# Lp-pooling over 1024 windows of four: one square and one sum per load, pairwise adds at the end, and an early first store

## The chip, the cores and the metric

The kernel runs on one core of a Trainium2 chip. Its time is the device time of one execution in microseconds (us); lower is better. "Span" is the time from the first to the last instruction of an execution; the device time of the kernel before is about 1.8 us longer.

## The reference

The input has 32 x 256 x 4096 float32 values (134.2 MB). Each output is the root of the mean of four neighbouring squares; the output has 32 x 256 x 1024 values (33.6 MB).

```python
window = np.abs(x[:, :, start:end]) ** p            # p = 2, four values
result[:, :, i] = (np.mean(window, axis=-1)) ** (1.0 / p)
```

## The kernel before

The flat input is cut into 22 loads; each has 128 rows, and most have 13184 columns (6.75 MB). Three SBUF slots hold loads, so two are usually on their way while one is worked on. Such a load is worked on in three chunks (the smaller loads at the end in two): ScalarE squares a chunk in place, VectorE sums each four neighbours with one `tensor_reduce`, and ScalarE takes the root one chunk later. Results of two loads form a group, with one store (at the end there is one group of three loads and one of a single load). Groups 0 to 6 are stored from ScalarE's queue; groups 7 to 10 are "late": they are stored from SyncE's (SP) queue, behind the last load.

```python
W, O_W = 13184, 6592
X_SLOTS, O_SLOTS = 3, 2
slots = [[(W, [4416, 4384, 4384])]] * 18
slots += [[(6592, [3296, 3296])] * 2, [(6592, [3296, 3296]), (5056, [2528, 2528])]]
groups = [2] * 9 + [3, 1]
late = {7, 8, 9, 10}
in_x = {9, 10}          # these results lie in a slot that no load needs any more
# ... cut: offsets, pools, load(), store()
def root(g, o, ends):
    nc.scalar.activation(out=o, in_=o, func=Act.Sqrt, scale=1.0 / k)
    if ends and g not in late:
        store(g, nc.scalar)
# ... cut: for each load i, with further loads issued up to two slots ahead
    for step in chunks:
        v = xs[i][:, c:c + step]
        nc.scalar.activation(out=v, in_=v, func=Act.Square)
        o = ots[g][:, at + c // k:at + (c + step) // k]
        nc.vector.tensor_reduce(
            out=o, in_=v.rearrange("p (n j) -> p n j", j=k),
            axis=mybir.AxisListType.X, op=mybir.AluOpType.add,
        )
        if pending is not None:
            root(*pending)
        c += step
        pending = (g, o, i == firsts[g] + groups[g] - 1 and c == w)
root(*pending)
for g in sorted(late):
    store(g, nc.sync)
```

## Time and profile before

| | kernel before |
|---|---|
| device time, median of the first 3 runs | 394.89 us (394.77 to 394.97) |
| span of the profiled run | 393.0 us |
| bytes moved, mean rate over the span | 167.79 MB, 427 GB/s |
| VectorE, ScalarE busy | 282.4 us, 292.4 us |

DVE is VectorE, ACT is ScalarE, SP is SyncE, which here only issues DMAs. The page of the kernel before, with the busy time of each engine (share of the span, number of instructions), the DMA's rate in 40 equal slices, and the memory traffic:

```profile
span 393.0 us, 316 instructions
## 1 busy us (share of the span) xinstructions
DVE 282.4 (72%) x62; ACT 292.4 (74%) x126; POOL 0.2 (0%) x4
...
GB/s 344 429 429 440 429 424 381 443 459 429 413 440 435 429 427 432 429 440 441 437 448 421 432 462 435 392 429 472 429 413 451 425 429 429 424 429 427 438 429 329
...
HBM read 134.22 MB, written 33.55 MB: 427 GB/s over the span
...
```

Only the first and the last slice are low; the bytes are fixed by the input and the output. Next, busy time by stretches, kernel before (start and end in us, length, then busy us and instructions of each engine, clock, DMA share, GB/s):

```profile
...
core 0: us, DVE busy (x) ACT busy (x) POOL busy (x), PEclk, DMA share, GB/s
4.00:388.00 384.00, 282.36 (x62) 291.15 (x125) 0.00 (x0) 1.00 1.00 432
340.00:388.00 48.00, 43.61 (x12) 43.16 (x23) 0.00 (x0) 1.00 1.00 431
388.00:390.00 2.00, 0.00 (x0) 0.00 (x0) 0.00 (x0) 1.00 0.89 376
390.00:392.00 2.00, 0.00 (x0) 0.00 (x0) 0.00 (x0) 1.00 0.52 215
392.00:394.00 2.00, 0.00 (x0) 0.00 (x0) 0.00 (x0) 1.00 0.00 0
...
```

The rate is 432 GB/s through the whole middle and 431 at the end, so I read no stage as having a limit other than the DMA. Three lines of the timeline of the kernel before (start, duration, engine, line, operation, tiles and shapes, number of instructions merged, and what ended the idle time):

```profile
...
19.53 7.63 ACT L108 ACTIVATE xt<-xt 128x4416 f32<-128x4416 f32 x2 [17.52 <-DMA xt<-in_x_dram]
...
35.10 3.88 ACT L108 ACTIVATE xt<-xt 128x4416 f32<-128x4416 f32 x1 [0.75 <-DMA xt<-in_x_dram]
...
50.70 3.88 ACT L108 ACTIVATE xt<-xt 128x4416 f32<-128x4416 f32 x1 [1.02 <-DMA xt<-in_x_dram]
...
```

ScalarE starts when a load has landed, at 19.53, 35.10 and 50.70 us, one 6.75 MB load every 15.6 us. From the groups of instructions by shape (output shape, input shape, count; busy us, mean ns of one; idle time before them):

```profile
...
L110 DVE TENSOR_REDUCE ot<-xt 128x1096 f32<-128x4384 f32 x36 | 169.9, 4719 | 6.7 <-ACT xt L108 6.4
L108 ACT ACTIVATE xt<-xt 128x4384 f32<-128x4384 f32 x36 | 138.3, 3843 | 2.9 <-ACT ot L84 2.9
...
```

The last DMA issues of SP, from the timeline of the kernel before; "x2" merges two, one at the start and one at the end of the piece:

```profile
...
342.45 0.80 SPq L75 DMA_DIRECT2D xt<-in_x_dram  x2
343.30 16.29 SPq L81 DMA_DIRECT2D out_dram<-ot  x2
381.39 6.11 SPq L81 DMA_DIRECT2D out_dram<-xt  x2
```

So the four late stores are issued at 343.3, 359.2, 381.4 and 387.2 us. The chain that ended last, from the page of the kernel before:

```profile
...
DMA 62%; ACT 19%; DVE 14%; issue 2%; ACTq 0%; SPq 0%
DMA xt<-in_x_dram 62%; ACT xt L108 15%; DVE ot L110 11%; DVE xt L110 3%; ACT ot L84 3%; ACT xt L84 1%; ACTq L81 0%; SPq L75 0%; ACTq L108 0%
...
```

It names ScalarE and VectorE for a third of the span. The chain follows what released the last instruction; it doesn't say that shorter work would have ended earlier. The stretches above say that the DMA had no pause to give.

### The profile page before, as it was taken

What the parts mean: (1) busy time and instruction counts of PE and PEld (TensorE: products, weight loads), DVE (VectorE), ACT (ScalarE), POOL (GpSimd) and SP (SyncE); (2) the same over time, 40 slices, a digit from 0 to 9 for tenths busy, and PEclk for the clock granted to TensorE, in tenths of its full rate; (3) what the DMA queues carried; (4) which work ended last, traced back from release to release, by engine and by line L of the source; (5) the groups of instructions that cost most, each with busy time, mean ns of one, the idle gap of its engine ahead of it and who ended that gap; (6) DMA issues with size and microseconds to landing.
All of it is one profiled execution on the core that took longest, in us unless ns stands there. A gap on an engine that the chain in (4) does not pass through costs nothing.

```text
span 393.0 us, 316 instructions
## 1 busy us (share of the span) xinstructions
DVE 282.4 (72%) x62; ACT 292.4 (74%) x126; POOL 0.2 (0%) x4
## 2 busy tenths in 40 slices
DVE  0068989494959495949594959595859686899992
ACT  1099986777786768686958695959595949899991
POOL 0000000000000000000000000000000000000000
DMA  8999999999999999999999999999999999999997
GB/s 344 429 429 440 429 424 381 443 459 429 413 440 435 429 427 432 429 440 441 437 448 421 432 462 435 392 429 472 429 413 451 425 429 429 424 429 427 438 429 329
DMA packets 4754, 167.79 MB, mean 427 GB/s; under 512 B 528, under 2 KB 528, under 8 KB 656
## 3 DMA queue, kind: packets, MB, share of 16 engines
q1 hardware_dynamic: 3744, 144.15, 85.3%
q10 hardware_dynamic: 1008, 23.63, 14.0%
q14 instruction: 2, 0.02, 0.0%
HBM read 134.22 MB, written 33.55 MB: 427 GB/s over the span
## 4 chain that ended last, share of the span: by engine, by line
DMA 62%; ACT 19%; DVE 14%; issue 2%; ACTq 0%; SPq 0%
DMA xt<-in_x_dram 62%; ACT xt L108 15%; DVE ot L110 11%; DVE xt L110 3%; ACT ot L84 3%; ACT xt L84 1%; ACTq L81 0%; SPq L75 0%; ACTq L108 0%
## 5 line engine op out<-in xcount | busy, mean ns | idle before, releaser
L110 DVE TENSOR_REDUCE ot<-xt 128x1096 f32<-128x4384 f32 (+1 forms) x54 | 255.4, 4731 | 102.7 <-ACT xt L108 102.4
L108 ACT ACTIVATE xt<-xt 128x4384 f32<-128x4384 f32 (+3 forms) x62 | 230.3, 3716 | 89.2 <-DMA xt<-in_x_dram 86.3
L84 ACT ACTIVATE ot<-ot 128x1096 f32<-128x1096 f32 (+1 forms) x54 | 59.8, 1108 | 1.8 <-DVE ot L110 0.9
L110 DVE TENSOR_REDUCE xt<-xt 128x824 f32<-128x3296 f32 (+1 forms) x8 | 27.0, 3384 | 1.3 <-ACT xt L108 1.2
L84 ACT ACTIVATE xt<-xt 128x824 f32<-128x824 f32 (+1 forms) x8 | 6.7, 841 | 3.0 <-DVE xt L110 2.9
L108 ACT ACT_TABLE_LOAD x1 | 1.3, 1283 | 0.7 <-PEq L137 0.7
L84 ACT ACT_TABLE_LOAD x1 | 1.3, 1283 | 0.0
L137 POOL MEMSET const-bfloat16-1.0<- 128x1 bf16 x1 | 0.1, 101 | 0.0
L137 POOL MEMSET const-uint8-127<- 128x1 uint8 x1 | 0.1, 101 | 0.0
L137 POOL MEMSET const-float32-0.0<- 128x1 f32 x1 | 0.1, 98 | 0.2 <-issue 0.2
L137 POOL MEMSET const-float32-1.0<- 128x1 f32 x1 | 0.1, 98 | 0.0
## 6 DMA issues: line engine op xcount, KB each, us to landing
xt<-in_x_dram SPq DMA_DIRECT2D x18, 6592.0 KB, 39.7
out_dram<-ot ACTq DMA_DIRECT2D x7, 3296.0 KB, 26.4
xt<-in_x_dram SPq DMA_DIRECT2D x3, 3296.0 KB, 24.6
out_dram<-ot SPq DMA_DIRECT2D x2, 3296.0 KB, 29.6
xt<-in_x_dram SPq DMA_DIRECT2D x1, 2528.0 KB, 26.4
out_dram<-xt SPq DMA_DIRECT2D x1, 2472.0 KB, 9.3
out_dram<-xt SPq DMA_DIRECT2D x1, 632.0 KB, 5.0
```

Source lines behind the costliest of these rows:

```text
L84: nc.scalar.activation(out=o, in_=o, func=Act.Sqrt, scale=1.0 / k)
L108: nc.scalar.activation(out=v, in_=v, func=Act.Square)
L110: nc.vector.tensor_reduce(out=o, in_=v.rearrange("p (n j) -> p n j", j=k), axis=mybir.AxisListType.X, op=mybir.AluOpType.add,)
L137: nc = _bacc.Bacc("TRN2", target_bir_lowering=False, num_devices=1)
```

## The change

The intent is fewer, larger instructions: one square and one sum for a whole load; from load 16 on, two packed pairwise adds instead of the reduce; roots by group; and an early start: the first 4416 columns are squared on VectorE beside ScalarE, and their 1104 results are stored from SP ahead of their group. The tiles become fixed buffers (that part of the diff is cut).

```diff
-    slots = [[(W, [4416, 4384, 4384])]] * 18
-    slots += [[(6592, [3296, 3296])] * 2, [(6592, [3296, 3296]), (5056, [2528, 2528])]]
+    slots = [[(W, [4416, 8768])]] + [[(W, [W])]] * 16 + [[(W, [6592, 6592])]]
+    slots += [[(6592, [6592]), (6592, [6592])], [(6592, [6592]), (5056, [2528, 2528])]]
-    in_x = {9, 10}
+    in_x = {9: (2, 0), 10: (2, 4944)}
+    FINE, ENDS, LAG = {21}, {19}, 1
+    PAIRS = 16
 ...
+        elif g == 0 and not stored[g]:
+            store(g, nc.sync, o.shape[1])
+    def total_sum(o, v, i):
+        if i < PAIRS: ...            # the tensor_reduce, as before
+        q = v.rearrange("p (n j) -> p n j", j=k)
+        front = v[:, 0:v.shape[1] // 2]
+        h = front.rearrange("p (n j) -> p n j", j=2)
+        nc.vector.tensor_tensor(out=h, in0=q[:, :, 0:2], in1=q[:, :, 2:4], op=add)
+        nc.vector.tensor_tensor(out=o, in0=h[:, :, 0], in1=h[:, :, 1], op=add)
 ...
-            nc.scalar.activation(out=v, in_=v, func=Act.Square)
-            ... tensor_reduce, then root(*pending)
+            if i == 0 and c == 0:
+                nc.vector.tensor_tensor(out=v, in0=v, in1=v, op=mybir.AluOpType.mult)
+            else:
+                nc.scalar.activation(out=v, in_=v, func=Act.Square)
+            total_sum(ots[g][:, summed:summed + step // k], v, i)
+            while pending and pending[0][0] <= done - LAG:
+                root(*pending.pop(0)[1:])
 ...
+            ends = summed == columns[g] // k
+            if ends or i in FINE or (i == 0 and c == step) or (i in ENDS and c == w):
+                pending.append((done - 1, g, ots[g][:, rooted:summed], ends))
```

More of the change, by code (lines that the diff above doesn't have):

```diff
@@ L55 @@
                for g in range(len(groups))]
-    x_pool = ctx.enter_context(tc.tile_pool(name="x_pool", bufs=X_SLOTS))
-    o_pool = ctx.enter_context(tc.tile_pool(name="o_pool", bufs=O_SLOTS))
+    x_pool = ctx.enter_context(tc.tile_pool(name="x_pool", bufs=1))
+    o_pool = ctx.enter_context(tc.tile_pool(name="o_pool", bufs=1))
+    x_tiles = [x_pool.tile([P, W], fp32, name=f"xt{j}") for j in range(X_SLOTS)]
+    o_tiles = [o_pool.tile([P, O_W], fp32, name=f"ot{j}") for j in range(O_SLOTS)]
     ctx.enter_context(tc.manual_schedule())
@@ L63, in block @@
         return flat[at:at + width].rearrange("(p w) -> p w", p=P)
-    slot_tiles = {}
     xs = {}
@@ L69, in load @@
         s, at, w, _ = loads[i]
-        if at == 0:
-            slot_tiles[s] = x_pool.tile([P, W], fp32, name="xt")
-        v = slot_tiles[s][:, at:at + w]
+        v = x_tiles[s % X_SLOTS][:, at:at + w]
         g = group_of[i]
@@ L78, with store @@
     ots = {}
-    def store(g, queue):
-        queue.dma_start(out=block(of, g, k), in_=ots[g])
+    stored = [0] * len(groups)
+    def store(g, queue, end=None):
+        first, end = stored[g], columns[g] // k if end is None else end
+        queue.dma_start(out=block(of, g, k)[:, first:end], in_=ots[g][:, first:end])
+        stored[g] = end
     def root(g, o, ends):
@@ L86, in root @@
             store(g, nc.scalar)
+        elif g == 0 and not stored[g]:
+            store(g, nc.sync, o.shape[1])
+    def total_sum(o, v, i):
+        add = mybir.AluOpType.add
+        if i < PAIRS:
+            nc.vector.tensor_reduce(
+                out=o, in_=v.rearrange("p (n j) -> p n j", j=k),
+                axis=mybir.AxisListType.X, op=add,
+            )
+            return
+        q = v.rearrange("p (n j) -> p n j", j=k)
[3 more added lines that the diff above has]
+        nc.vector.tensor_tensor(out=o, in0=h[:, :, 0], in1=h[:, :, 1], op=add)
     ahead = 0
@@ L91 @@
         ahead += 1
-    pending = None
+    pending = []
+    done = 0
     for i in range(n):
@@ L99 @@
         if i == firsts[g]:
-            pool, width = (o_pool, O_W) if g not in in_x else (x_pool, W)
-            t = pool.tile([P, width], fp32, name="ot" if g not in in_x else "xt")
-            ots[g] = t[:, 0:columns[g] // k]
-        at = sum(loads[j][2] for j in range(firsts[g], i)) // k
+            t, first = (o_tiles[g % O_SLOTS], 0) if g not in in_x else (x_tiles[in_x[g][0]], in_x[g][1])
+            ots[g] = t[:, first:first + columns[g] // k]
+            summed = rooted = 0
         assert sum(chunks) == w
@@ L107 @@
             v = xs[i][:, c:c + step]
-            nc.scalar.activation(out=v, in_=v, func=Act.Square)
-            o = ots[g][:, at + c // k:at + (c + step) // k]
-            nc.vector.tensor_reduce(
-                out=o, in_=v.rearrange("p (n j) -> p n j", j=k),
-                axis=mybir.AxisListType.X, op=mybir.AluOpType.add,
-            )
-            if pending is not None:
-                root(*pending)
-            c += step
-            pending = (g, o, i == firsts[g] + groups[g] - 1 and c == w)
-    root(*pending)
+            if i == 0 and c == 0:
[5 more added lines that the diff above has]
+                root(*pending.pop(0)[1:])
+            done += 1
+            c += step
+            summed += step // k
+            ends = summed == columns[g] // k
+            if ends or i in FINE or (i == 0 and c == step) or (i in ENDS and c == w):
+                pending.append((done - 1, g, ots[g][:, rooted:summed], ends))
+                rooted = summed
+    for job in pending:
+        root(*job[1:])
     for g in sorted(late):
```

## The prediction

> What bounds the kernel now: the DMA, over the whole span. The page counts 167.79 MB in 393.0 us. The view of busy time by stretches gives 432 GB/s from 4 to 388 us at a DMA share of 1.00, 431 from 20 to 340 and from 340 to 388: no stage is slower. The timeline shows ScalarE starting on loads at 19.53, 35.10 and 50.70 us, one 6.75 MB load per 15.6 us (433 GB/s). The Trainium skill ("DMA: Bandwidth & Descriptors", section "Where 436 GB/s comes from") puts the ceiling at 435; the trace agrees within 1%.
>
> The chain of waits names ScalarE and VectorE for the last 47 us, but I read the end as DMA-bound too. The last stores are issued at 343.3, 359.2, 381.4 and 387.2 us; the last two land 9.3 and 5.0 us later, at 390.7 and 392.2. The second lands near 384.8 (landing median of the first two 29.6). So 2.53 MB takes 5.9 us and 0.65 MB 1.5, exactly the DMA rate: the stores stand in a queue, and the last results are ready 3.5 us before it reaches them.
>
> Floor: start 3.9 us (19.53 minus 15.6) plus 167.8 MB at 432 GB/s = 388.4 makes 392.3; the last store lands at 392.2. Nothing is left outside the DMA.
>
> What changes:
> - One square per load instead of three: 3 x 3.85 becomes about 11.2 us (slope 0.836 ns per column between the forms of 3296 and 4384). A slot is freed about 25 us after its load lands (11.2 square, 13.9 sum) instead of 18. Loads land every 19.6 us with two in flight, so the next load is still issued some 14 us before the queue runs dry.
> - First 4416 columns squared on VectorE (about 4.7 us): VectorE ends slot 0 near 38 us, as now. Their store, 0.57 MB, goes out near 30 us. It moves bytes forward in a queue that is full already, gaining nothing.
> - Packed pairwise adds in loads 16 to 21: two tensor_tensor instead of one reduce. The Trainium skill ("VectorE: DVE Perf Modes", section "The perf-mode tier table") has fp32 tensor_tensor at 1x, so I estimate 0.75 of the reduce: 6592 columns 5.3 us instead of 7.0.
> - Tail by my hand schedule: roots end near 386 to 387 us (now 387.15); store 9 ready near 381 to 382, store 10 near 386 to 387. Both find the queue occupied (until 384.8 and 390.7).
>
> On the critical path: none of it, to within 0.3 us. Bytes and DMA rate are unchanged.
>
> Predicted: 394.8 us, 8 in 10 within 393.9 to 395.9. Faster by over 2%: 0.01; within 2%: 0.96; slower by over 2%: 0.03.
>
> Signs that I am right: 431 to 433 GB/s from 4 to 388 us; first load used at 19.5; ScalarE and VectorE busy time down (VectorE by about 10 us net) with the span within 1 us; last stores landing back to back. Signs that a step is wrong: a stretch of several us under 420 GB/s (slots freed too late); pair adds over 0.8 of the reduce; the last store issued after its predecessor has landed.
>
> What would make it wrong: strided pair adds at half speed, which would push the tail by up to 10 us; false waits between reused tiles (the early store holding VectorE, stores holding later sums), draining the load queue; a DMA rate that depends on how reads and writes overlap, worth 1 us either way.

## The result

| | before | changed |
|---|---|---|
| device time, median of 6 runs | 394.92 us (394.77 to 395.22) | 395.65 us (395.36 to 395.86) |
| span of the profiled run | 393.0 us | 394.0 us |
| VectorE, ScalarE busy | 282.4, 292.4 us | 269.5, 277.9 us |

The ratio is 1.0017 (95% interval 1.0004 to 1.003). The page of the changed kernel, the same parts as before:

```profile
span 394.0 us, 198 instructions
## 1 busy us (share of the span) xinstructions
DVE 269.5 (68%) x34; ACT 277.9 (71%) x40; POOL 0.2 (0%) x4
...
GB/s 343 428 428 428 428 400 428 450 462 402 428 452 431 455 434 404 431 471 428 391 439 455 426 428 428 431 428 463 431 455 396 471 434 428 388 428 433 429 433 283
...
HBM read 134.22 MB, written 33.55 MB: 426 GB/s over the span
...
```

VectorE works 12.9 us less and ScalarE 14.5 us less, and the span of the profiled run is 1 us longer. Busy time by stretches, changed kernel:

```profile
...
4.00:388.00 384.00, 269.45 (x34) 276.61 (x39) 0.00 (x0) 1.00 1.00 432
340.00:388.00 48.00, 37.74 (x16) 44.74 (x13) 0.00 (x0) 1.00 1.01 433
388.00:390.00 2.00, 0.00 (x0) 0.00 (x0) 0.00 (x0) 1.00 0.88 372
390.00:392.00 2.00, 0.00 (x0) 0.00 (x0) 0.00 (x0) 1.00 0.42 172
392.00:394.00 2.00, 0.00 (x0) 0.00 (x0) 0.00 (x0) 1.00 0.02 8
...
```

From 4 to 388 us the DMA rate is again 432 GB/s. The timeline of the changed kernel, at the start:

```profile
...
19.50 7.51 ACT L134 ACTIVATE xt<-xt 128x8768 f32<-128x8768 f32 x1 [17.49 <-DMA xt<-in_x_dram]
19.50 4.76 DVE L132 TENSOR_TENSOR xt<-xt 128x4416 f32<-128x4416 f32 x1 [19.50 <-DMA xt<-in_x_dram]
...
30.23 0.35 SPq L86 DMA_DIRECT2D out_dram<-ot  x1
35.08 11.19 ACT L134 ACTIVATE xt<-xt 128x13184 f32<-128x13184 f32 x1 [4.87 <-DMA xt<-in_x_dram]
38.27 39.06 SPq L77 DMA_DIRECT2D xt<-in_x_dram  x3
...
```

The first load is used at 19.50 us on both engines at once, and the early store is issued at 30.23 us (by the trace's packet records its bytes move from 50.1 to 52.9 us, behind loads that stood in the queue already). The first slot is free again, and its next load is issued, at 38.27 us; before it was 38.12 us. The groups by shape, changed kernel:

```profile
...
L99 DVE TENSOR_REDUCE ot<-xt 128x3296 f32<-128x13184 f32 x15 | 208.3, 13886 | 80.2 <-ACT xt L134 80.2
L134 ACT ACTIVATE xt<-xt 128x13184 f32<-128x13184 f32 x16 | 179.0, 11190 | 87.8 <-DMA xt<-in_x_dram 86.6 <-ACT ot L90 1.2
...
L108 DVE TENSOR_TENSOR xt<-xt 128x3296 f32<-128x3296 f32 x5 | 18.0, 3593 | 6.5 <-ACT xt L134 6.3
...
L109 DVE TENSOR_TENSOR xt<-xt 128x1648 f32<-128x1648 f32 x3 | 5.6, 1874 | 0.1
L132 DVE TENSOR_TENSOR xt<-xt 128x4416 f32<-128x4416 f32 x1 | 4.8, 4759 | 19.5 <-DMA xt<-in_x_dram 19.5
...
```

The pairwise adds of 6592 columns take 3.59 + 1.87 = 5.47 us; the reduce of the same width took 7.01 us (measured in the run without pair adds, below). The last issues of SP, changed kernel:

```profile
...
346.01 0.80 SPq L77 DMA_DIRECT2D xt<-in_x_dram  x2
346.90 16.75 SPq L86 DMA_DIRECT2D out_dram<-ot  x2
381.63 5.65 SPq L86 DMA_DIRECT2D out_dram<-xt  x2
```

Store 9 is issued at 381.63 us and store 10 at 386.95 us, 0.24 us later and 0.22 us earlier than before.

Where, then, is the longer span? Every DMA reports its completion 16 times, once for each of the 16 DMA engines that share it. For the last store, in us from the start of the span, taken from the trace's completion records:

```
                       median engine   mean engine   last engine   last minus median
before                       391.62        391.63        392.22              0.60
changed                      391.29        391.46        393.12              1.83
changed, second run          391.33        391.41        392.60              1.26
```

The median and the mean engine end up to 0.3 us earlier than before. The last engine ends 0.4 to 0.9 us later, and the span ends with it. (The records don't name the engine, so it need not be the same one throughout.) In the changed kernel the last engine was 0.86 us behind the median at the first load, 1.26 us at the first load after the early store and 1.8 to 1.9 us from about 210 us on, apart from landings with another transfer in between. As long as the queue doesn't run empty, I read a lag as staying, unless the others lose time too; experiments 7 to 9, where the queue runs empty, bear this out (last section).

The step at the early store stands in all nine kept traces that have three slots and such a store: the lag grows by 0.16 to 0.54 us between the landings just before and just after its bytes. But it belongs to the first store of a run, early or not: in the three traces without an early store (before, experiments 1 and 2) the lag stays or falls there and grows by 0.2 to 0.4 us at their first store. The kernels part later: before, the lag falls by 0.5 us between 83 and 90 us; in the changed kernel it grows by another 0.66 us near 210 us, in experiment 2 by 1.0 us between 144 and 165 us. The traces show no cause for these steps.

### The profile page after: what moved, and what is told of

Its sections match the earlier page's. It is cut to its first block, busy times and chain, and to the rows that moved or that the text cites. A ratio compares the mean times of both kernels' runs of the same rounds, so it can differ in the third digit from the quotient of the medians.

```text
span 394.0 us, 198 instructions
## 1 busy us (share of the span) xinstructions
DVE 269.5 (68%) x34; ACT 277.9 (71%) x40; POOL 0.2 (0%) x4
## 4 chain that ended last, share of the span: by engine, by line
DMA 43%; ACT 28%; DVE 16%; issue 11%; ACTq 0%; SPq 0%
DMA xt<-in_x_dram 43%; ACT xt L134 20%; DVE ot L99 14%; ACT ot L90 7%; DVE xt L108 1%; DVE xt L109 1%; ACT xt L90 1%; ACTq L86 0%; SPq L77 0%; ACTq L90 0%
## 5 line engine op out<-in xcount | busy, mean ns | idle before, releaser
L134 ACT ACTIVATE xt<-xt 128x13184 f32<-128x13184 f32 (+3 forms) x24 | 219.2, 9147 | 105.3 <-DMA xt<-in_x_dram 104.1
L99 DVE TENSOR_REDUCE ot<-xt 128x3296 f32<-128x13184 f32 (+2 forms) x17 | 222.2, 13078 | 80.3 <-ACT xt L134 80.2
L90 ACT ACTIVATE ot<-ot 128x6592 f32<-128x6592 f32 (+2 forms) x10 | 51.3, 5134 | 0.8 <-DVE ot L99 0.8
L108 DVE TENSOR_TENSOR xt<-xt 128x3296 f32<-128x3296 f32 (+2 forms) x8 | 27.9, 3492 | 16.7 <-ACT xt L134 16.4
L132 DVE TENSOR_TENSOR xt<-xt 128x4416 f32<-128x4416 f32 x1 | 4.8, 4759 | 19.5 <-DMA xt<-in_x_dram 19.5
L90 ACT ACTIVATE xt<-xt 128x632 f32<-128x632 f32 (+2 forms) x4 | 6.0, 1493 | 2.2 <-DVE xt L109 2.1
L109 DVE TENSOR_TENSOR ot<-xt 128x1648 f32<-128x1648 f32 (+1 forms) x3 | 7.3, 2447 | 0.1
L109 DVE TENSOR_TENSOR xt<-xt 128x1648 f32<-128x1648 f32 (+1 forms) x5 | 7.3, 1452 | 0.2
```

Source lines behind the costliest of these rows:

```text
L99: nc.vector.tensor_reduce(out=o, in_=v.rearrange("p (n j) -> p n j", j=k), axis=mybir.AxisListType.X, op=add,)
L108: nc.vector.tensor_tensor(out=h, in0=q[:, :, 0:2], in1=q[:, :, 2:4], op=add)
L109: nc.vector.tensor_tensor(out=o, in0=h[:, :, 0], in1=h[:, :, 1], op=add)
L132: nc.vector.tensor_tensor(out=v, in0=v, in1=v, op=mybir.AluOpType.mult)
```

## The experiments

"Before" in each line is the kernel before, run on the same chip.

**1. The DMA alone.** All loads and stores stay, but the arithmetic handles only the last 64 columns of a chunk. The results are wrong (relative error 0.58); the result tiles are filled once at the start. There is no early store.

```diff
-nc.scalar.activation(out=v, in_=v, func=Act.Square)
+nc.scalar.activation(out=v[:, step - 64:step], in_=v[:, step - 64:step], func=Act.Square)
# sums and roots in the same way on the last 16 results
```

> The changed kernel with its arithmetic cut to the last 64 columns of each chunk (wrong result on purpose) and without the early store; every load and store keeps its bytes, its queue and its place in the order. If the DMA alone sets the time of both kernels: within 1 us of the kernel before (394.0 to 395.9). If the chain of ScalarE and VectorE at the end, or the late release of slots, sets it: at least 2 us shorter (under 393).

Measured: 394.73 us (4 runs), before 394.73 (9 runs), ratio 0.9998 (0.9983 to 1.0014). The page of this run:

```profile
span 393.2 us, 208 instructions
## 1 busy us (share of the span) xinstructions
DVE 17.7 (5%) x36; ACT 10.3 (3%) x40; POOL 0.2 (0%) x4
...
```

With 18 us of VectorE and 10 us of ScalarE left, the time is the same. Without the early store, the loads and stores of this run have the bytes, queues and order of the kernel before. So the kernel before is at the floor of its DMA pattern, to within the 0.7 us that the interval leaves; the rival (that the chain of engines at the end costs time) falls for it.

**2. No early store.** The two lines of the early store are taken out. The first 1104 results still get their own root; they are stored with their group.

```diff
-        elif g == 0 and not stored[g]:
-            store(g, nc.sync, o.shape[1])
```

> The changed kernel without the early store: the first 4416 columns are still squared on VectorE, their sums are rooted and stored with their group. If the early store causes the 0.7 us (it puts one of the 16 DMA engines further behind, the others waiting for nothing): 394.8 to 395.1, spread of the last store's completions over the engines about 1 us. If the coarse squares, the later stores they bring, or chance cause it: 395.4 to 395.8, spread about 2 us.

Measured: 395.59 us, before 394.73, ratio 1.0023 (1.001 to 1.0035). The last engine was 1.62 us behind the median. So the early store is not the whole cause: without it the time does not come back. There is a trap in this number: the device time is 2.3 us above the span in all five runs, against 1.73 to 1.82 us for the kernel before and 1.85 to 1.95 us for the changed kernel. The spans themselves are 393.2 to 393.4 us. About 0.5 us of this run's 0.86 us thus lies outside the span.

**3. Early store alone.** The kernel before, with the early store from SP added and nothing else.

> The kernel before with one thing added: the first 1104 results of group 0 are stored on the SP queue as soon as they are rooted. If the early store costs the 0.7 us: 395.4 to 395.8, spread of the last store's completions about 2 us. If not: 394.8 to 395.1, spread about 1 us.

Measured: 395.11 us, before 394.73, ratio 1.0011 (0.9998 to 1.0023), last engine 1.19 us behind the median. It lies between the two expectations: by itself this run tells little, the store may cost some 0.4 us, or nothing.

**4. The changed kernel again.**

> The changed kernel, nothing altered, a second time. If its 0.7 us belongs to the kernel: 395.4 to 395.8 again and a spread of the last completions of about 2 us. If it was that chip or those runs: within 0.3 us of the kernel before.

Measured: 395.35 us, before 394.73, ratio 1.0015 (1.0002 to 1.0028). The difference is there in a second set of runs, so it belongs to the kernel and not to those runs; its size moves by a few tenths. (This set ran on chip 14; the record doesn't say on which chip the first one did, so chips are not compared.)

**5. The DMA alone, with the early store.** As experiment 1, with the two lines of the early store kept.

> The DMA of the changed kernel alone, as in the run with the arithmetic cut down, but with the early store of 0.57 MB in place. If the early store (128 more rows, of 4.4 KB) costs something in the DMA itself: 395.0 to 395.5, 0.3 us or more above the 394.7 without it. If it is free: 394.5 to 394.9.

Measured: 395.26 us (394.8 to 395.53), before 394.92, ratio 1.0007 (0.9995 to 1.002). The five runs lie on both sides of the line drawn. Against its own "before" each, the early store reads as 0.34 us here (experiment 1 has 0.00) and as 0.38 us in experiment 3; each interval reaches zero. A few tenths are possible and not shown.

**6. Fine chunks in the changed kernel.**

```diff
-slots = [[(W, [4416, 8768])]] + [[(W, [W])]] * 16 + [[(W, [6592, 6592])]]
+slots = [[(W, [4416, 4384, 4384])]] * 18
```

> The changed kernel with loads 0 to 17 squared and summed in three chunks each, as in the kernel before; early store, VectorE's first square, pair adds and roots by group stay. If the coarse squares and sums (slots freed 25 us after landing instead of 18, stores issued later) cost the time: span back to about 393.0 us and the time to 394.7 to 395.0. If the cost is chance among the 16 DMA engines or lies in the stores: 395.1 to 395.6 with a span of 393.2 to 393.6.

Measured: 395.37 us, before 394.92, ratio 1.0012 (0.9999 to 1.0026), spans 393.2 to 393.9 us. So the coarse chunks are at most a small part of the few tenths.

**7. The reduce to the end.** `PAIRS = 22`, so no load uses pair adds.

> The changed kernel with the one-instruction reduce kept to the end, no pair adds. VectorE should be about 13 us busier and the last root a little later (387 to 390 us instead of 386.9). If the end is bound by the queue of stores: within 0.3 us of the changed kernel (395.1 to 395.7). If VectorE's tail sets the end: 1 us or more above it (over 396.3).

Measured: 400.90 us, before 394.92, ratio 1.0154 (1.014 to 1.0168). The second case holds: it is 5.5 us above the changed kernel's 395.35 us of experiment 4. Busy time by stretches of this run:

```profile
...
380.00:384.00 4.00, 4.00 (x2) 3.08 (x2) 0.00 (x0) 1.00 0.78 336
384.00:388.00 4.00, 4.00 (x2) 2.22 (x2) 0.00 (x0) 1.00 0.00 0
388.00:390.00 2.00, 2.00 (x1) 2.00 (x2) 0.00 (x0) 1.00 0.00 0
...
```

The view counts a packet in the stretch in which it starts. By the packet records, the 16 engines end the earlier stores between 383.16 and 384.70 us, and no further data moves until 390.28 us, 0.84 us after store 9 is issued at 389.44 us: here the queue of stores does run dry. The waits of this run (engine and line, what it waited for; us in total, times, longest):

```profile
...
ACT ot L90 <- DVE ot L99: 6.2, 2, 5.5
DVE xt L99 <- ACT xt L134: 5.6, 2, 4.4
...
```

The same in its timeline:

```profile
...
362.43 7.01 DVE L99 TENSOR_REDUCE xt<-xt 128x1648 f32<-128x6592 f32 x1
362.55 5.70 ACT L90 ACTIVATE ot<-ot 128x6592 f32<-128x6592 f32 x1 [5.46 <-DVE ot L99]
...
373.86 16.64 DVE L99 TENSOR_REDUCE xt<-xt 128x1648 f32<-128x6592 f32 x3 [4.42 <-ACT xt L134]
...
```

ScalarE stands 5.5 us before the root of group 8, because the sum of load 17 isn't done; behind it in ScalarE's order stands the square of load 19, and VectorE then waits 4.4 us for that square.

**8. The fourth corner: fine chunks and the reduce.** Experiment 6 with `PAIRS = 22`.

> The fourth corner: the changed kernel with loads 0 to 17 in three chunks and the one-instruction reduce to the end. If the 5.5 us that the coarse kernel loses without pair adds are VectorE's backlog from starting each sum only after a whole 13184-column square: 396 to 397, because by hand schedule the last store is then ready near 391 us, some 1.5 us after the queue runs dry, instead of 394.5 to 395. If the reduce itself costs the 5.5 us whatever the chunks: 400 to 401.

Measured: 399.11 us, before 394.64, ratio 1.0113 (1.0098 to 1.0129). It falls between both expectations. Each against its own "before", the loss is 4.5 us here and 6.0 us in experiment 7, so the chunks of loads 0 to 17 are worth 1.5 us of it. I read the rest as coming from what the kernel before doesn't have and this one still has: whole sums of 6592 columns in loads 18 to 20, and one root for a whole group. The next experiment tests the second.

**9. The reduce, with the last roots later.** Experiment 7, but from load 17 on a root is issued one square later, so ScalarE squares the next load before it waits.

```diff
-while pending and pending[0][0] <= done - LAG:
+while pending and pending[0][0] <= done - (LAG if i < 17 else 2):
```

> The kernel with coarse chunks and the reduce to the end (400.9 us), with one thing changed: from load 17 on a root is issued two squares after its own sum's square instead of one, so ScalarE squares the next load before it waits for VectorE. If the loss is the two engines waiting for each other at the end (ScalarE 5.5 us for the sum of load 17, then VectorE 4.4 us for the square of load 19): VectorE works without a break from 335 us, the last but one store is ready near 385 us, when the queue runs dry, and the last near 389.5; so 394.7 to 395.8, as the changed kernel with pair adds. If it is the bare time of the reduces: 400 to 401.

Measured: 396.47 us, before 394.78, ratio 1.0043 (1.0029 to 1.0057). This order alone takes back 4.4 of the 5.5 us (400.90 to 396.47), with not one VectorE instruction made faster. VectorE now works without a break from 334.84 to 388.74 us. The stretches of this run:

```profile
...
380.00:384.00 4.00, 4.00 (x2) 2.22 (x2) 0.00 (x0) 1.00 0.80 343
384.00:388.00 4.00, 4.00 (x2) 1.69 (x2) 0.00 (x0) 1.00 0.56 237
388.00:390.00 2.00, 0.74 (x1) 0.73 (x1) 0.00 (x0) 1.00 1.11 475
...
```

What is left is a short dry spell: store 9 is issued at 384.99 us, and by the packet records the 16 engines were done with the earlier stores between 383.31 and 384.77 us; its first data moves at 385.82 us.

**10. Pair adds in every load.** `PAIRS = 0`.

> The changed kernel with pair adds in every load, so VectorE is some 55 us less busy. If only the end depends on VectorE and the DMA sets the rest: within 0.3 us of the changed kernel, 395.1 to 395.7. If VectorE's time or the earlier release of slots (by 3.5 us) counts in the middle: 394.8 or less.

Measured: 395.49 us, before 394.64, ratio 1.0017 (1.0005 to 1.003), the same as the changed kernel. VectorE's time in the middle is worth nothing, as expected.

**11 and 12. Two slots instead of three,** with coarse and with fine chunks. These ask whether the early release of slots matters at all.

```diff
-v = x_tiles[s % X_SLOTS][:, at:at + w]
+v = x_tiles[s % LIVE][:, at:at + w]        # LIVE = 2, also in the two loops that issue ahead
```

> The changed kernel with two slots for loads instead of three (the third tile only keeps the last results). A slot is then asked for again 25 us after its load landed, while the other slot's load takes some 20 us with the stores in the way: the DMA should stand still 5 to 8 us per load, so I expect 90 to 140 us more (485 to 535 us). If the release of slots did not matter at all: under 400 us.

Measured: 460.18 us (2 runs), before 394.92, ratio 1.1655. The stretch from 60 to 150 us of this run:

```profile
...
60.00:150.00 90.00, 51.83 (x5) 51.55 (x6) 0.00 (x0) 1.00 0.89 369
...
```

> Two slots as in the run with two slots and coarse chunks (460 us), now with loads 0 to 17 in three chunks: a slot is freed about 18 us after its load landed instead of 25. If the release of slots sets the stall: about 7 us less in each stalled load, and half the loads stall, so 400 to 425 us. If the stall comes from elsewhere: still near 460.

Measured: 429.80 us (2 runs), before 394.64, ratio 1.089, a little above the range given. In both runs the direction is right and the sizes were not: with coarse chunks two loads take 46.7 us (ScalarE begins on loads at 83.26 and, two loads later, at 129.92 us) instead of 39.1 us at 432 GB/s, so two loads lose 7.6 us together, and I had reckoned with a loss in every load. The packet records have one pause of all engines in every two loads there (6.0 us from 103.3 us). Chunks of a third save 30 us here. With three slots the same chunks save nothing, because another load still stands in the queue: in the changed kernel a slot is asked for again at 288.58 us, and the load ahead of it lands at about 301.6 us.

## Why the prediction was right

- *The DMA bounds the whole span; nothing is left outside it.* Shown by experiment 1 (ratio 0.9998 with the arithmetic gone) and by the same 432 GB/s in both kernels.
- *None of the change is on the critical path, 394.8 us.* The measured 395.65 us lies inside 393.9 to 395.9, near its upper end. "To within 0.3 us" did not hold: the prediction had no term for the 0.7 us (0.6 in the second set) that are clear of noise in two sets of runs, and that they fit into the range is owed to its width. About 0.1 us of them lies outside the span. The rest shows in the last of the 16 DMA engines, not in the median one. Why one engine falls further behind is not settled: without the early store, with fine chunks, or with pair adds in every load, the kernel stayed 0.45 to 0.86 us above its "before".
- *Slots freed at 25 instead of 18 us do no harm.* Right: no stretch lost rate against the kernel before (432 GB/s from 60 to 340 us in both; 411 against 405 from 40 to 60 us, where both are low). The margin of 14 us was 13 us at the place checked late in the run; experiments 11 and 12 show what happens without it.
- *The early store gains nothing.* Right; there is no gain in any run.
- *Pair adds at 0.75 of the reduce.* Measured 5.47 against 7.01 us, 0.78. The Trainium skill ("VectorE: DVE Perf Modes", section "The TRN2 errata — SBUF-src ops pay a fixed extra latency per instruction") gives (N+151)/0.96 ns for an fp32 `tensor_tensor`: 3591 ns for N = 3296. The trace agrees: 3593 ns for the first add, which reads pairs four columns apart, and 1874 ns at N = 1648 for the second, which reads every second column.
- *Last results ready 3.5 us before the queue reaches them.* The tail came as scheduled by hand (stores issued at 381.63 and 386.95 us), but this term was mis-sized. I compared an issue with a landing. By the packet and completion records, data moves 0.83 to 0.84 us after an issue when the queue is dry (experiments 7, 8 and 9), and a landing is reported 0.4 to 0.5 us after the last packet ends. (The Trainium skill, "DMA: Bandwidth & Descriptors", section "Anatomy of one DMA — SWDGE (gpsimd) path", puts most of a fixed cost of about 2 us into that receipt, for DMAs issued from GpSimd; for these, issued from SP, the records show less.) Before, the engines ended the earlier stores between 383.34 and 384.31 us. Store 9 was issued at 381.39 us, so, with the 0.83 us of the dry queue, it could have come 1.1 us later before the first engine ran dry, and about 2 us before the last one did. The last one counts: in experiments 7, 8 and 9 store 9 was issued 8.05, 6.26 and 3.60 us later than before, and their spans are 6.1, 4.3 and 1.7 us longer, always about 2 us less. So the slack of the kernel before was about 2 us and not 3.5. In the changed kernel, issued at 381.63 us with engines ending between 383.16 and 385.21 us, it was 0.7 us for the first engine and 2.7 us for the last, by the same estimate.
- *On the critical path: none of it.* The prediction treated each part as worth nothing. For the whole this holds, but the parts do not stand alone: coarse sums and roots by group would have cost 5.5 us at the end (experiment 7), and the pair adds are what pays for it. The change spends a slack that it must then buy back.

## What to carry to other kernels

When a run with the arithmetic cut away takes the same time as the kernel, stop tuning the arithmetic; only bytes, transfer rate and the two ends remain. Larger instructions are not free even then: they lengthen the path from the last load to the last store, and in an engine that works in order, a root that waits for the other engine holds up the square behind it. That order alone was worth 4.4 us in experiment 9, nearly as much as the 5.5 us of the faster pair adds. Judge slack at a queue by when data stops flowing on the engine that ends last, not by when a landing is reported.

## What the Trainium skill lacked or had wrong

- "DMA: Bandwidth & Descriptors": it says that a load runs at the pace of its slowest engine, but not that an engine's lag is mostly carried along while the queue stays full, and vanishes when it runs dry. Here the last engine ended 0.60 to 1.83 us behind the median in the kernels whose queue never ran dry, and 0.08 to 0.11 us behind in experiments 7, 8 and 9, where it did.
- "SBUF — State Buffer", its summary of rules, wants 358 GB/s for HBM to SBUF. For a core running alone that is too low: this one moved 432 GB/s, loads and stores together. "HBM Reference" is nearer with 425 GB/s for a core alone.
- No page that I read has it: the transfers just before the first store of a run are slow. Nearly all packets of 52.7 KB took 1.95 to 1.96 us, but in the changed kernel one on each of the 16 engines took 2.8 to 3.2 us, from 47.2 us on, just before the early store's bytes. Without the early store (experiment 2) the slow ones come at 68.6 us, just before the store that is then the first; the engines of the kernel before lost about 1 us each at their first store, spread over a few packets. (The first packets of each run are slow too, 2.2 to 3.2 us in the changed kernel.)
- "VectorE: DVE Perf Modes" has no duration for `tensor_reduce` by size. Here 4384 columns took 4719 ns and 13184 columns 13886 ns, which is 1.04 ns for each column more.
- No page that I read tells that device time minus span depends on the program: 1.73 to 1.82 us for the kernel before, 1.85 to 1.95 for the changed one, 2.3 for the one without the early store (spans to 0.1 us). What it depends on was not tested.
